# Mask tiles of a chunked recurrence: from 32 keys by 16 queries to 64 keys by 32 queries

## The chip, the cores and the metric

The kernel runs on one core of a Trainium2 chip. The metric is device time in microseconds (us) of one launch. TensorE is called PE here, VectorE DVE, ScalarE ACT, GpSimd POOL, SyncE SP. PEld is PE's weight load, which the profile lists beside the matmuls. The time before is 2788.95 us, the median of three runs (2788.55 to 2790.15).

## The reference

The reference is one step of a one-layer trunk: an RMS norm, a projection `x @ w_in` to nine groups of 1024 channels, a recurrence branch (HGRN2), a convolution branch (31 taps), two branch projections merged by gates, an output projection, and a gated embedding. It is computed for 2048 prompt tokens and for a sample group of 8 by 8 = 64 tokens. The change lies in the recurrence alone. For each of 8 heads, with 128 key channels:

```
S_t = diag(f_t) S_{t-1} + (1 - f_t) v_t^T          o_t = S_t^T q_t
attn[t, s] = sum_k q[t,k] (1 - f)[s,k] * prod_{s<u<=t} f[u,k]     for s <= t
o = attn @ v + (decayed q) @ S
```

`attn` is needed as blocks of 128 keys by 128 queries for prompt tokens, and as one 64 by 64 block for the sample group (eight independent sequences of 8 tokens).

## The kernel before, in words

**Stages.** The kernel runs, in order: the projection (`plan_head`, 8 heads in each of two token halves, up to about 1940 us), the two branch projections with the layer norm beside them (to about 2330 us), and the output stage. All large matmuls of the first two stages are issued at L1363, by a loop over units: a unit is one weight block against up to 512 tokens, 8 x 3 matmuls (the operands are split in a high and a low part). Behind each unit's 24 matmuls the loop issues whatever small jobs fall due in that unit. Due times are in units; `plan` of class `Hgrn` writes them by hand with `put(t, ...)`. Every engine works its own instructions in the order in which they are issued.

**The recurrence.** There are 32 `Hgrn` objects: 8 heads by 4 groups of 512 tokens. The last group of each head also carries the 64 sample tokens (`smp`), which makes 8 such objects and 24 without. The block of attention weights is built by doubling. Level h (1, 2, 4, ..., 64) joins each run of h keys with the h queries that follow it. DVE multiplies keys and queries of a level by their decays (`decay`, L436) and extends the running products (`grow`, L423). PE then forms the products over the 128 channels, and DVE copies the wanted entries out of PSUM under a mask (`evac_level`, L486).

**Tiles on PE before.** `mm_diag` (L448) takes 32 keys as weights against 32 queries. `mm_level` for h = 1 to 16 (L462) takes 32 keys as weights against the 16 queries of the same 32 tokens that are second halves. The four 32-token pieces of a chunk of 128 tokens write the output partitions 0, 32, 64 and 96 onward. For h = 32 two tiles of 32 by 32 a chunk, at output partitions 0 and 64, and for h = 64 one tile of 64 by 64 a chunk, at output partitions 0 to 63, are issued at L470. An output range of partitions is called a column strip in what follows: before, four strips of 32, and for h = 64 one strip of 64. Every f32 matmul of this kind has two records in the trace.

**Order.** `LVT` puts the matmuls of one object into three bursts: the diagonal with levels 1 and 2 (due at 2.0 units after the object's start), levels 4, 8 and 16 (4.25), levels 32 and 64 (5.4). The evacuations are due at 3.2 (diagonal, 1, 2), 4.9 (4, 8) and 5.85 (16). `gather` (ACT, L494 to L503) is due at 6.6 and copies the finished blocks into `at`, which `mm_o` at 9.0 uses as weights.

**Buffers.** PSUM tile `d32p` holds the diagonal and levels 1 to 8 of all chunks, `ab` holds level 16, 32 and 64. SBUF tile `d32` collects the 32 by 32 blocks (the trace names it `d`).

Of the kernel before, what the change touches and what calls it, by code (L numbers as in the profile page):

```python
# [17 lines left out]
P = 128  # L18
# [7 lines left out]
G = 512  # L26
# [6 lines left out]
LVT = ((2.0, (1, 2)), (4.25, (4, 8, 16)), (5.4, (32, 64)))  # L33
# [41 lines left out]
def view(t, off, dims):  # L75
    return bass.AP(t.tensor, t.offset + off, [list(t.ap[0])] + [list(d) for d in dims])
# [7 lines left out]
def tile_hybrid_step(  # L84
# [7 lines left out]
    nc = tc.nc  # L92
# [33 lines left out]
    ident = const.tile([P, P], F32, name="ident")  # L126
# [108 lines left out]
    oml = c1.tile([P, NH], F32, name="oml")  # L235
    lmx = c1.tile([P, NH], F32, name="lmx")
    cw = c1.tile([P, KB, 32], F32, name="cw")
    dmask = c1.tile([P, 32], F32, name="dmask")
    smask = c1.tile([NS, 8], F32, name="smask")
    lmask = {h: c1.tile([P, 16], I32, name=f"lmask{h}") for h in (1, 2, 4, 8, 16)}  # L240

    def bias(kind, j):
        c = UNIT_OF[kind] * 8 + j
# [26 lines left out]
    def set_masks():  # L270
        nc.vector.memset(onest, 1.0 / D)
        nc.vector.tensor_reduce(
            out=dmask, in_=ident.rearrange("p (a t) -> p t a", t=32), axis=mybir.AxisListType.X, op=ALU.add)
        for h, m in lmask.items():
            nb = 16 // h
            red = c1.tile([P, 16], F32, name="red", tag="red", bufs=2)
            nc.vector.tensor_reduce(
                out=red[:, 0:nb], in_=dmask.rearrange("p (b e i) -> p b e i", e=2, i=h)[:, :, 0, :],
                axis=mybir.AxisListType.X, op=ALU.add)
            nc.vector.tensor_copy(  # L280
                m.rearrange("p (b i) -> p b i", i=h), red[:, 0:nb].unsqueeze(2).broadcast_to([P, nb, h]))
        nc.vector.tensor_reduce(
            out=smask, in_=ident[0:NS, 0:NS].rearrange("p (b i) -> p b i", i=8), axis=mybir.AxisListType.X, op=ALU.add)
# [3 lines left out]
    at = c1.tile([P, 4, P], F32, name="at")  # L287
    at_s = c1.tile([NS, NS], F32, name="at_s")
    qm = c1.tile([P, 8, NS], F32, name="qm")
    s_all = c1.tile([P, NH, P], F32, name="s_all")  # L290
    tails = c1.tile([P, NH, 30], F32, name="tails")
    d32p = ps_1.tile([P, 5, 96], F32, name="d32p")
    nc.vector.memset(d32p, 0.0)

    for t in (lvl[0], lvl[1], lvl[2], at, at_s, qm, tails):
        nc.vector.memset(t, 0.0)
# [13 lines left out]
    blocks = []  # L310
# [44 lines left out]
    def lvl_row(h):  # L355
        i = (h.bit_length() - 1) % 6
        return lvl[i // 2][:, i % 2, :]

    class Hgrn:


        def __init__(self, j, tok0, smp):
            self.j, self.tok0, self.smp = j, tok0, smp
            self.n = 576 if smp else 512
            self.m = 5 if smp else 4
            self.kq = self.rp = self.v = self.za = None

        def alloc_kq(self):
# [66 lines left out]
                a, b = (view(t, 0, [[576 + h, 2], [2 * h, nb], [1, h]]) for t in (self.kq, self.rp))  # L435
            nc.vector.tensor_tensor(out=o, in0=a, in1=b, op=ALU.mult)  # L436

        def chunks(self, h):
            for c in range(4):
                yield c, 4  # L440
            if self.smp and h <= 4:
                yield 4, 2

        def mm_diag(self):
            for c, nq in self.chunks(0):
                for b in range(nq):
                    o = P * c + 32 * b
                    nc.tensor.matmul(  # L448
                        d32p[32 * b:32 * b + 32, c, 0:32], lhsT=self.kq[:, 0, o:o + 32], rhs=self.kq[:, 1, o:o + 32],
                        start=True, stop=True)  # L450

        def mm_level(self, h):
            lv = lvl_row(h)
            kk = self.kq[:, 0, :] if h == 1 else lv
            if h == 16:
                self.ab = ps_1.tile([P, 4, P], F32, tag="ab", name="ab")
            if h <= 16:
                dst, s = (self.ab, 0) if h == 16 else (d32p, 16 + 16 * h.bit_length())
                for c, nq in self.chunks(h):
                    for b in range(nq):  # L460
                        o = P * c + 32 * b
                        nc.tensor.matmul(  # L462
                            dst[32 * b:32 * b + 32, c, s:s + 16], lhsT=kk[:, o:o + 32],
                            rhs=lv[:, o:o + 32].rearrange("p (a e i) -> p a e i", e=2, i=h)[:, :, 1, :],
                            start=True, stop=True)
            else:
                for c in range(4):
                    for b in range(64 // h):
                        o = 2 * h * b
                        nc.tensor.matmul(  # L470
                            self.ab[o:o + h, c, o + h:o + 2 * h], lhsT=lv[:, P * c + o:P * c + o + h],
                            rhs=lv[:, P * c + o + h:P * c + o + 2 * h], start=True, stop=True)

        def evac_diag(self):
            m = self.m
            self.d32 = h1.tile([P, 5, 32], F32, tag="d32", name="d32")
            nc.vector.tensor_tensor(
                out=self.d32[:, 0:m], in0=d32p[:, 0:m, 0:32], in1=dmask.unsqueeze(1).broadcast_to([P, m, 32]),
                op=ALU.mult)

        def evac_level(self, h):
            m = 4 if h > 4 else self.m
            nb = 16 // h
            src = (view(self.ab, 0, [[P, 4], [16, 1], [1, 16]]) if h == 16 else
                   view(d32p, 16 + 16 * h.bit_length(), [[96, m], [h, nb], [1, h]]))
            nc.vector.copy_predicated(  # L486
                view(self.d32, h, [[32, m], [2 * h, nb], [1, h]]),
                view(lmask[h], 0, [[0, m], [h, nb], [1, h]]),
                src)

        def gather(self):
            for b in range(4):
                r = slice(32 * b, 32 * b + 32)
                nc.scalar.activation(out=at[r, :, r], in_=self.d32[r, 0:4, :], func=AF.Copy)  # L494
            for b in range(2):
                nc.scalar.activation(
                    out=at[64 * b:64 * b + 32, :, 64 * b + 32:64 * b + 64],
                    in_=self.ab[64 * b:64 * b + 32, :, 64 * b + 32:64 * b + 64], func=AF.Copy)
            nc.scalar.activation(out=at[0:64, :, 64:P], in_=self.ab[0:64, :, 64:P], func=AF.Copy)
            if self.smp:  # L500
                for b in range(2):
                    r = slice(32 * b, 32 * b + 32)
                    nc.scalar.activation(out=at_s[r, r], in_=self.d32[r, 4, :], func=AF.Copy)  # L503

        def final(self):
            n = self.n
# [114 lines left out]
        def plan(self, t0, tv):  # L621

            smp = self.smp
            ev = []

            def put(t, *fns):
                for fn in fns:
                    at_time(t0 + t, fn, 0)

            put(0.0, self.prep)  # L630
            for i, h in enumerate((1, 2, 4, 8, 16, 32, 64)):
                put(0.75 * i, lambda h=h: self.decay(h), lambda h=h: self.grow(h))
            for t, hs in LVT:
                put(t, *([self.mm_diag] if 1 in hs else []), *(lambda h=h: self.mm_level(h) for h in hs))
            put(3.2, self.evac_diag, lambda: self.evac_level(1), lambda: self.evac_level(2))
            put(4.9, lambda: self.evac_level(4), lambda: self.evac_level(8))
            put(5.25, self.final)
            put(5.85, lambda: self.evac_level(16))
            put(6.35, self.k_turn)
            put(6.6, self.gather)  # L640
            put(7.3, self.mm_kv)
            put(8.2, self.chain)
            put(9.0, self.mm_o)
            put(9.9, self.norm_o)
            put(11.2, self.turn_o)
            if smp:
                put(KTS, self.k_turn_sample)
                put(7.5, self.sample_o)
# [271 lines left out]
    for which, w, times, ev in (("a", w_br_a, t_a, evac_a), ("b", w_br_b, t_b, evac_b)):  # L920
        for hf in range(2):
# [151 lines left out]
    for i in range(9):  # L1073
        t, b = XOUT0 + XOUT_STEP * i, 8 + i
# [255 lines left out]
    for t, prio, n, fn in todo:  # L1330
        i = min(bisect.bisect_right(clock, t + 1e-6) - 1, len(units) - 1)
# [5 lines left out]
    for b in range(1, len(blocks)):  # L1337
        i = 1 if b == 2 else max(uses[b][0] - 3, 0)
# [133 lines left out]
```

## Time and profile before

| | us |
|---|---|
| median of 3 runs | 2788.95 |
| the profiled execution, its own time | 2788.37 |
| its span (first to last instruction) | 2786.6 |
| PE busy | 2754.3 |
| PE weight load busy | 2371.3 |
| DVE busy | 1943.8 |
| ACT busy | 931.4 |
| POOL busy | 283.4 |

1.8 us of the execution's time lie outside the span. The granted TensorE clock over the span is 0.998 of full speed. A busy share says how much of a stretch an engine had an instruction in flight. Matmuls overlap each other, so their mean durations are longer than the time that one adds; what one adds is read from the distance between starts.

### The profile page before, as it was taken

What the parts mean: (1) busy time and instruction counts of PE and PEld (TensorE: products, weight loads), DVE (VectorE), ACT (ScalarE), POOL (GpSimd) and SP (SyncE); (2) the same over time, 40 slices, a digit from 0 to 9 for tenths busy, and PEclk for the clock granted to TensorE, in tenths of its full rate; (3) what the DMA queues carried; (4) which work ended last, traced back from release to release, by engine and by line L of the source; (5) the groups of instructions that cost most, each with busy time, mean ns of one, the idle gap of its engine ahead of it and who ended that gap; (6) DMA issues with size and microseconds to landing.
All of it is one profiled execution on the core that took longest, in us unless ns stands there. A gap on an engine that the chain in (4) does not pass through costs nothing. (4 is left out here: it accounts for less than half of the span.)

```text
span 2786.6 us, 50684 instructions
## 1 busy us (share of the span) xinstructions
PE 2754.3 (99%) x21199; PEld 2371.3 (85%) x21199; DVE 1943.8 (70%) x3242; ACT 931.4 (33%) x2119; POOL 283.4 (10%) x441
## 2 busy tenths in 40 slices
PE   7999999999999999999999999999999999999998
PEld 6888888888888898989888998989889788788887
DVE  6577787877778787677778777688877775333433
ACT  5333333333333432223322323233254443322222
POOL 2001000000000000000000000000046410000000
PEclk9999999999999999999999999999999999999999
DMA  4222222222221422122222222123687788422321
GB/s 124 63 72 80 77 85 86 85 84 73 73 69 61 134 62 82 57 73 75 79 67 64 81 61 84 53 86 107 208 267 223 235 276 279 138 89 79 91 80 40
DMA packets 352797, 292.68 MB, mean 105 GB/s; under 512 B 17514, under 2 KB 301259, under 8 KB 352568
## 3 DMA queue, kind: packets, MB, share of 16 engines
q1 hardware_dynamic: 293856, 218.40, 26.0%
q10 hardware_dynamic: 58440, 70.86, 7.4%
q8 instruction: 166, 2.72, 0.4%
q14 instruction: 63, 0.52, 0.1%
q0 software_dynamic: 272, 0.19, 0.0%
HBM read 201.25 MB, written 88.14 MB: 104 GB/s over the span
## 5 line engine op out<-in xcount | busy, mean ns | idle before, releaser
L703 DVE SCALAR_TENSOR_TENSOR acc<-u,cw,acc 128x512 f32<-128x512 f32 x960 | 734.1, 765 | 20.7
L1363 PE MATMUL mm<-x1h,whi 128*128 128x320 f32 (+2 forms) x2112 | 708.2, 335 | 0.0
L1363 PE MATMUL mm<-x1h,wlo 128*128 128x320 f32 (+2 forms) x2112 | 691.1, 327 | 0.0
L1363 PE MATMUL mm<-x1l,whi 128*128 128x320 f32 (+2 forms) x2112 | 690.8, 327 | 0.0
L1363 PE MATMUL mm<-x0h,whi 128*128 128x512 f32 (+1 forms) x1416 | 563.3, 398 | 1.9 <-ACT x0h L1037 1.1
L1363 PE MATMUL mm<-x0l,whi 128*128 128x512 f32 (+1 forms) x1416 | 551.8, 390 | 1.8 <-DVE x0l L176 1.5
L1363 PE MATMUL mm<-x0h,wlo 128*128 128x512 f32 (+1 forms) x1416 | 551.7, 390 | 0.0
L1363 PEld LDWEIGHTS mm<-x1h,whi 128*128 128x128 f32 x2112 | 399.3, 189 | 33.8 <-ACT rp L376 4.5
L1363 PEld LDWEIGHTS mm<-x1h,wlo 128*128 128x128 f32 x2112 | 398.8, 189 | 28.2
L1363 PEld LDWEIGHTS mm<-x1l,whi 128*128 128x128 f32 x2112 | 399.4, 189 | 26.3
L327 DVE TENSOR_TENSOR wlo<-raw,whi 128x1024 fp32r<-128x1024 f32 x176 | 216.5, 1230 | 227.5 <-ACT whi L326 221.5
L1363 PEld LDWEIGHTS mm<-x0h,whi 128*128 128x128 f32 x1416 | 266.6, 188 | 59.3 <-ACT sp L786 2.6
L1363 PEld LDWEIGHTS mm<-x0h,wlo 128*128 128x128 f32 x1416 | 266.6, 188 | 57.0 <-DVE wlo L327 0.4
L1363 PEld LDWEIGHTS mm<-x0l,whi 128*128 128x128 f32 x1416 | 267.0, 189 | 53.3 <-DVE x0l L176 2.1
L326 ACT ACTIVATE whi<-raw 128x1024 fp32r<-128x1024 f32 x176 | 186.0, 1057 | 70.9 <-DVE mal L895 32.0
L1194 PE MATMUL ps<-woh,mgi 128*128 128x512 f32 x528 | 168.4, 393 | 2.0 <-DMA mgi<-mg_dr 2.0
L423 DVE TENSOR_TENSOR rp<-rp 128x512 f32<-128x512 f32 (+1 forms) x224 | 156.8, 700 | 9.6
L436 DVE TENSOR_TENSOR lvl<-kq,rp 128x512 f32<-128x512 f32 (+2 forms) x224 | 146.6, 655 | 1.9
L1194 PEld LDWEIGHTS ps<-woh,mgi 128*128 128x128 f32 x528 | 99.1, 188 | 22.9 <-DMA mgi<-mg_dr 2.2
L786 ACT ACTIVATE sp<-mm,vcol 128x512 f32<-128x512 f32 (+2 forms) x120 | 73.0, 608 | 130.8 <-PE mm L1363 117.2
L1268 DVE TENSOR_TENSOR g<-ps,g 128x512 f32<-128x512 f32 x32 | 22.1, 692 | 133.4 <-ACT g L1267 128.6
L567 POOL TENSOR_SCALAR ors<-oss 128x4 f32<-128x4 f32 (+1 forms) x40 | 10.7, 266 | 973.2 <-ACT on L565 973.2
(253 smaller groups left out, 3277.9 us busy)
## 6 DMA issues: line engine op xcount, KB each, us to landing
raw<-in_w_in_dram SPq DMA_DIRECT2D x144, 512.0 KB, 3.9
mgi<-mg_dr SPq DMA_DIRECT2D x16, 1024.0 KB, 6.1
gate<-am_dr SPq DMA_DIRECT2D x24, 512.0 KB, 5.7
mg_dr<-mg SPq DMA_DIRECT2D x24, 512.0 KB, 3.4
xt<-in_x_prompt_dram SPq DMA_DIRECT2D x16, 512.0 KB, 5.0
g_dr<-gst ACTq DMA_DIRECT2D x32, 256.0 KB, 2.8
cv_dr<-acc ACTq DMA_DIRECT2D x32, 256.0 KB, 2.1
raw<-in_w_br_a_dram SPq DMA_DIRECT2D x16, 512.0 KB, 5.4
```

Source lines behind the costliest of these rows:

```text
L326: nc.scalar.activation(out=b.hi, in_=b.raw, func=AF.Copy)
L327: nc.vector.tensor_tensor(out=b.lo, in0=b.raw, in1=f32(b.hi), op=ALU.subtract)
L423: nc.vector.tensor_tensor(out=io, in0=io, in1=tt, op=ALU.mult)
L436: nc.vector.tensor_tensor(out=o, in0=a, in1=b, op=ALU.mult)
L567: nc.gpsimd.tensor_scalar(out=rs[0:n, 0:m], in0=ss[0:n, 0:m], scalar1=1.0 / P, scalar2=EPS, op0=ALU.mult, op1=ALU.add)
L703: nc.vector.scalar_tensor_tensor(out=self.acc, in0=self.u[:, i:i + G], scalar=w, in1=self.acc, op0=ALU.mult, op1=ALU.add)
L786: nc.scalar.activation(out=s[:, 0:n], in_=ps[:, 0:n], func=func, bias=bias(kind, j))
L1194: nc.tensor.matmul(ps, lhsT=a[:, k, :], rhs=c[:, k, s], start=(k == 0 and i == 0), stop=(k == kn - 1 and i == len(ops) - 1))
L1268: nc.vector.tensor_tensor(out=g[0:n], in0=pp[0:n], in1=g[0:n], op=ALU.mult)
L1363: nc.tensor.matmul(ps[:, 0:u.n], lhsT=w[:, k, :], rhs=x[:, k, sl], start=(k == 0 and w is u.block.hi and x is xh), stop=(k == KB - 1 and w ...
```

## The change

Tiles of a level become 64 keys by 32 queries, tiles of the diagonal 64 by 64, and levels 1 to 32 go this way; h = 64 keeps its tile. A chunk of 128 tokens then has two pieces, at output partitions 0 and 64: two column strips of 64. The blocks are collected as 64 by 64 in `d`, so that `gather` copies two diagonal blocks and the h = 64 corner of a chunk instead of four blocks, two level-32 corners and the h = 64 corner. The masks `dmask` and `lmask` widen to 64 and 32 columns with one more level. The PSUM tiles become two full banks: `da` (diagonal, level 2, later 32 and 64) and `ab` (levels 1, 4, 8, 16, and the sample's diagonal, 1 and 2), and `ab` is taken at `mm_diag` instead of at level 16. The sample's level 4 is issued apart, with the third burst. The sample's evacuations are separate instructions. The set-up no longer clears `d32p`. The program is also built with `dynamic_dma_scratch_size=8192`. The due times of the bursts stay; level 32 joins level 16 in the evacuation at 5.85.

```
-        def chunks(self, h):
-            for c in range(4):
-                yield c, 4
-            if self.smp and h <= 4:
-                yield 4, 2
+        def blocks(self, h):
+            for c in range(4):
+                for b in range(2):
+                    yield P * c + 64 * b, 64 * b, c
+            if self.smp and h <= 4:
+                yield 512, 0, 4
+        def place(self, h, c):
+            if c == 4:
+                return ((da, 384) if h == 4 else (self.ab, {0: 384, 1: 448, 2: 480}[h]))
+            at, base = {0: (da, 0), 1: (da, 256), 2: (da, 384), 4: (self.ab, 0), 8: (self.ab, 128), 16: (self.ab, 256),
+                        32: (da, 0), 64: (da, 128)}[h]
+            return at, base + (32 if 0 < h < 64 else 64) * c
         def mm_diag(self):
...
+            for o, r, c in self.blocks(0):
+                bank, s = self.place(0, c)
+                nc.tensor.matmul(
+                    bank[r:r + 64, s:s + 64], lhsT=self.kq[:, 0, o:o + 64], rhs=self.kq[:, 1, o:o + 64],
+                    start=True, stop=True)
         def mm_level(self, h):
...
+            for o, r, c in self.blocks(h):
+                if c == 4 and h == 4:
+                    continue
+                bank, s = self.place(h, c)
+                if h < 64:
+                    nc.tensor.matmul(
+                        bank[r:r + 64, s:s + 32], lhsT=kk[:, o:o + 64],
+                        rhs=lv[:, o:o + 64].rearrange("p (a e i) -> p a e i", e=2, i=h)[:, :, 1, :],
+                        start=True, stop=True)
+                elif r == 0:
+                    nc.tensor.matmul(
+                        bank[0:64, s:s + 64], lhsT=lv[:, o:o + 64], rhs=lv[:, o + 64:o + P], start=True, stop=True)
...
+        def evac_level(self, h, c=0):
+            nb = 32 // h
+            n, m = (64, 1) if c == 4 else (P, 4)
+            bank, s = self.place(h, c)
             nc.vector.copy_predicated(
+                view(self.d[0:n], 64 * c + h, [[64, m], [2 * h, nb], [1, h]]),
+                view(lmask[h][0:n], 0, [[0, m], [h, nb], [1, h]]),
+                view(bank[0:n], s, [[32, m], [h, nb], [1, h]]))
...
+            put(LVT[2][0], self.mm_sample_4)
+            put(3.2, self.evac_diag, lambda: self.evac_levels((1, 2), (1, 2)))
+            put(4.9, lambda: self.evac_levels((4, 8), ()))
             put(5.25, self.final)
-            put(5.85, lambda: self.evac_level(16))
+            put(5.85, lambda: self.evac_levels((16, 32), (4,)))
```

## Rows read from the trace of the kernel before

**Rows 1.** The page: busy time of each engine with its share of the span and its instructions, and the granted TensorE clock in 40 equal slices of the span, in tenths.

```profile
PE 2754.3 (99%) x21199; PEld 2371.3 (85%) x21199; DVE 1943.8 (70%) x3242; ACT 931.4 (33%) x2119; POOL 283.4 (10%) x441
...
PEclk9999999999999999999999999999999999999999
```

**Rows 2.** Busy time of each engine in five stretches that cover the span: start, first and second half of the projection stage, branch projections, output stage. Columns: the stretch, its length, then busy us (and instructions) of PE, PEld, DVE, ACT and POOL, clock, DMA share, GB/s.

```profile
0.00:55.00 55.00, 41.00 (x218) 34.50 (x219) 38.93 (x70) 33.77 (x65) 15.55 (x40) 0.94 0.44 138
55.00:1000.00 945.00, 945.00 (x7978) 787.50 (x7977) 703.41 (x1067) 318.86 (x679) 50.17 (x76) 1.00 0.26 79
1000.00:1940.00 940.00, 940.00 (x8885) 845.50 (x8884) 720.52 (x1231) 288.30 (x678) 63.44 (x72) 1.00 0.24 72
1940.00:2330.00 390.00, 382.61 (x2040) 332.48 (x2040) 304.50 (x539) 163.25 (x346) 122.58 (x151) 1.00 0.78 247
2330.00:2786.60 456.60, 445.74 (x2087) 371.36 (x2085) 176.49 (x339) 127.25 (x352) 31.69 (x102) 1.00 0.33 102
```

**Rows 3.** Who waited for whom, PE's waits, the two longest: us in total, times, longest.

```profile
PE xtr L172 <- DVE xt L160: 11.7, 4, 9.2
PE rs L1016 <- POOL diag L1008: 5.3, 2, 4.9
```

**Rows 4.** Groups of instructions by line with shapes kept apart, PE, the matmuls of the mask over the whole span: weights as rows*columns, moving operand as partitions x columns, count of records | busy us, mean ns of one | idle before.

```profile
L462 PE MATMUL d32p<-lvl 128*32 128x16 f32 x3136 | 39.1, 185 | 0.0
...
L470 PE MATMUL ab<-lvl 128*64 128x64 f32 x256 | 21.7, 228 | 0.0
...
L462 PE MATMUL d32p<-lvl,kq 128*32 128x16 f32 x1056 | 15.4, 186 | 0.0
L448 PE MATMUL d32p<-kq 128*32 128x32 f32 x1056 | 15.2, 199 | 0.0
L462 PE MATMUL ab<-lvl 128*32 128x16 f32 x1024 | 14.9, 185 | 0.0
L470 PE MATMUL ab<-lvl 128*32 128x32 f32 x512 | 14.2, 199 | 0.0
```

**Rows 5.** Timeline of PE, the first burst of one object without sample tokens, between the last large matmul ahead of it and the first behind it. Columns here and in rows 6 to 9: start in us, us from the first start to the last end of the merged records, engine, line, operation, tiles, shapes, records.

```profile
93.59 0.39 PE L1363 MATMUL mm<-x0h,wlo 128*128 128x512 f32 x1
93.91 0.46 PE L448 MATMUL d32p<-kq 128*32 128x32 f32 x32
...
94.49 0.43 PE L462 MATMUL d32p<-lvl 128*32 128x16 f32 x30
94.86 0.50 PE L1363 MATMUL mm<-x0h,whi 128*128 128x512 f32 x1
```

**Rows 6.** The same view of the second burst of the same object.

```profile
107.26 0.39 PE L1363 MATMUL mm<-x1h,wlo 128*128 128x512 f32 x1
107.58 0.71 PE L462 MATMUL d32p<-lvl 128*32 128x16 f32 x62
...
108.51 0.50 PE L1363 MATMUL mm<-x1h,whi 128*128 128x512 f32 x1
```

**Rows 7.** The same view of a third burst, asked in narrow stretches so that single records stand apart: the 16 records of level 32, then the first, the second with the three after it, and the last of the 8 records of level 64, then the next large matmul.

```profile
806.83 0.45 PE L470 MATMUL ab<-lvl 128*32 128x32 f32 x16
...
807.20 0.27 PE L470 MATMUL ab<-lvl 128*64 128x64 f32 x1
807.31 0.40 PE L470 MATMUL ab<-lvl 128*64 128x64 f32 x4
...
807.66 0.22 PE L470 MATMUL ab<-lvl 128*64 128x64 f32 x1
807.81 0.50 PE L1363 MATMUL mm<-x1h,whi 128*128 128x512 f32 x1
```

**Rows 8.** The same view of an object with sample tokens: the first rows of its first and second burst, each with the large matmul behind the burst.

```profile
1006.10 0.53 PE L448 MATMUL d32p<-kq 128*32 128x32 f32 x36
...
1007.18 0.50 PE L1363 MATMUL mm<-x0h,whi 128*128 128x512 f32 x1
...
1020.10 0.77 PE L462 MATMUL d32p<-lvl 128*32 128x16 f32 x68
...
1021.08 0.39 PE L1363 MATMUL mm<-x1h,whi 128*128 128x256 f32 x1
```

**Rows 9.** Timeline of PE's weight loads in the layer norm's variance sum, whose matmuls have a single moving column: two neighbouring loads of 128 weight columns, then the two loads of 64 weight columns that follow.

```profile
2221.62 0.19 PEld L995 LDWEIGHTS vr<-onest,sum 128*128 128x128 f32 x1
2221.73 0.19 PEld L995 LDWEIGHTS vr<-onest,sum 128*128 128x128 f32 x1
...
2221.94 0.13 PEld L995 LDWEIGHTS vr<-onest,sum 128*64 128x64 f32 x1
2221.99 0.14 PEld L995 LDWEIGHTS vr<-onest,sum 128*64 128x64 f32 x1
```

**Rows 10.** The evacuations: two groups by line and shape on DVE (busy us, mean ns of one | idle before), the instructions of tile `d32p` that form the diagonal (min/median/max ns, first and last start), one group on ACT, and DVE's wait at the third burst.

```profile
L486 DVE COPY_PREDICATED d<-lmask,d32p 128x64 f32<-128x64 int32 x104 | 27.4, 263 | 30.4 <-PE d32p L462 27.6
...
L486 DVE COPY_PREDICATED d<-lmask,d32p 128x80 f32<-128x80 int32 x24 | 7.3, 303 | 0.6
...
L477 DVE TENSOR_TENSOR d<-d32p,dmask x32: 282/284/318, 57.0 to 1910.7; 128x128 f32<-128x128 f32 x24, 128x160 f32<-128x160 f32 x8
...
L494 ACT ACTIVATE at<-d 32x128 f32<-32x128 f32 x128 | 39.1, 305 | 8.1 <-DVE wlo L327 5.3 <-DVE d L486 1.6
...
DVE d L486 <- PE ab L470: 84.4, 15, 6.5
```

More of the change, by code (lines that the diff above doesn't have):

```diff
@@ L237, in tile_hybrid_step @@
     cw = c1.tile([P, KB, 32], F32, name="cw")
-    dmask = c1.tile([P, 32], F32, name="dmask")
+    dmask = c1.tile([P, 64], F32, name="dmask")
     smask = c1.tile([NS, 8], F32, name="smask")
-    lmask = {h: c1.tile([P, 16], I32, name=f"lmask{h}") for h in (1, 2, 4, 8, 16)}
+    lmask = {h: c1.tile([P, 32], I32, name=f"lmask{h}") for h in (1, 2, 4, 8, 16, 32)}
     def bias(kind, j):
@@ L272, in set_masks @@
         nc.vector.tensor_reduce(
-            out=dmask, in_=ident.rearrange("p (a t) -> p t a", t=32), axis=mybir.AxisListType.X, op=ALU.add)
+            out=dmask, in_=ident.rearrange("p (a t) -> p t a", t=64), axis=mybir.AxisListType.X, op=ALU.add)
         for h, m in lmask.items():
-            nb = 16 // h
-            red = c1.tile([P, 16], F32, name="red", tag="red", bufs=2)
+            nb = 32 // h
+            red = c1.tile([P, 32], F32, name="red", tag="red", bufs=2)
             nc.vector.tensor_reduce(
@@ L291, in tile_hybrid_step @@
     tails = c1.tile([P, NH, 30], F32, name="tails")
-    d32p = ps_1.tile([P, 5, 96], F32, name="d32p")
-    nc.vector.memset(d32p, 0.0)
+    da = ps_1.tile([P, G], F32, name="da")
     for t in (lvl[0], lvl[1], lvl[2], at, at_s, qm, tails):
@@ L364, in __init__ @@
             self.n = 576 if smp else 512
-            self.m = 5 if smp else 4
             self.kq = self.rp = self.v = self.za = None
@@ L436, in decay @@
             nc.vector.tensor_tensor(out=o, in0=a, in1=b, op=ALU.mult)
-        def chunks(self, h):
+        def blocks(self, h):
             for c in range(4):
-                yield c, 4
+                for b in range(2):
+                    yield P * c + 64 * b, 64 * b, c
             if self.smp and h <= 4:
-                yield 4, 2
-        def mm_diag(self):
[L445 to L450, printed above, removed]
+                yield 512, 0, 4
[5 more added lines that the diff above has]
+            return at, base + (32 if 0 < h < 64 else 64) * c
+        def mm_diag(self):
+            self.ab = ps_1.tile([P, G], F32, tag="ab", name="ab")
+            for o, r, c in self.blocks(0):
[3 more added lines that the diff above has]
+                    start=True, stop=True)
         def mm_level(self, h):
@@ L454, in mm_level @@
             kk = self.kq[:, 0, :] if h == 1 else lv
[L455 to L466, printed above, removed]
-                for c in range(4):
[L468 to L472, printed above, removed]
+            for o, r, c in self.blocks(h):
[10 more added lines that the diff above has]
+                        bank[0:64, s:s + 64], lhsT=lv[:, o:o + 64], rhs=lv[:, o + 64:o + P], start=True, stop=True)
@@ L474, in evac_diag, with mm_sample_4 @@
+        def mm_sample_4(self):
+            if self.smp:
+                bank, s = self.place(4, 4)
+                lv = lvl_row(4)[:, 512:576]
+                nc.tensor.matmul(
+                    bank[0:64, s:s + 32], lhsT=lv,
+                    rhs=lv.rearrange("p (a e i) -> p a e i", e=2, i=4)[:, :, 1, :], start=True, stop=True)
         def evac_diag(self):
-            m = self.m
-            self.d32 = h1.tile([P, 5, 32], F32, tag="d32", name="d32")
+            self.d = h1.tile([P, 5, 64], F32, tag="d", name="d")
@@ L477, in evac_diag @@
             nc.vector.tensor_tensor(
[L478 to L485, printed above, removed]
-            nc.vector.copy_predicated(
-                view(self.d32, h, [[32, m], [2 * h, nb], [1, h]]),
-                view(lmask[h], 0, [[0, m], [h, nb], [1, h]]),
-                src)
+                out=self.d[:, 0:4], in0=da[:, 0:256].rearrange("p (c t) -> p c t", c=4),
@@ new lines, in evac_diag @@
+                in1=dmask.unsqueeze(1).broadcast_to([P, 4, 64]), op=ALU.mult)
+            if self.smp:
+                nc.vector.tensor_tensor(
+                    out=self.d[0:64, 4], in0=self.ab[0:64, 384:448], in1=dmask[0:64], op=ALU.mult)
+        def evac_level(self, h, c=0):
+            nb = 32 // h
+            n, m = (64, 1) if c == 4 else (P, 4)
+            bank, s = self.place(h, c)
+            nc.vector.copy_predicated(
+                view(self.d[0:n], 64 * c + h, [[64, m], [2 * h, nb], [1, h]]),
+                view(lmask[h][0:n], 0, [[0, m], [h, nb], [1, h]]),
+                view(bank[0:n], s, [[32, m], [h, nb], [1, h]]))
@@ L491, in gather, with evac_levels @@
+        def evac_levels(self, hs, sample):
+            for h in hs:
+                self.evac_level(h)
+            for h in sample if self.smp else ():
+                self.evac_level(h, 4)
         def gather(self):
-            for b in range(4):
-                r = slice(32 * b, 32 * b + 32)
-                nc.scalar.activation(out=at[r, :, r], in_=self.d32[r, 0:4, :], func=AF.Copy)
             for b in range(2):
-                nc.scalar.activation(
-                    out=at[64 * b:64 * b + 32, :, 64 * b + 32:64 * b + 64],
-                    in_=self.ab[64 * b:64 * b + 32, :, 64 * b + 32:64 * b + 64], func=AF.Copy)
@@ L499, in gather @@
-            nc.scalar.activation(out=at[0:64, :, 64:P], in_=self.ab[0:64, :, 64:P], func=AF.Copy)
+                r = slice(64 * b, 64 * b + 64)
+                nc.scalar.activation(out=at[r, :, r], in_=self.d[r, 0:4, :], func=AF.Copy)
+            nc.scalar.activation(
+                out=at[0:64, :, 64:P], in_=da[0:64, 128:384].rearrange("p (c t) -> p c t", c=4), func=AF.Copy)
             if self.smp:
-                for b in range(2):
-                    r = slice(32 * b, 32 * b + 32)
-                    nc.scalar.activation(out=at_s[r, r], in_=self.d32[r, 4, :], func=AF.Copy)
+                nc.scalar.activation(out=at_s, in_=self.d[0:64, 4, :], func=AF.Copy)
@@ L634, in plan @@
                 put(t, *([self.mm_diag] if 1 in hs else []), *(lambda h=h: self.mm_level(h) for h in hs))
-            put(3.2, self.evac_diag, lambda: self.evac_level(1), lambda: self.evac_level(2))
-            put(4.9, lambda: self.evac_level(4), lambda: self.evac_level(8))
+            put(LVT[2][0], self.mm_sample_4)
+            put(3.2, self.evac_diag, lambda: self.evac_levels((1, 2), (1, 2)))
+            put(4.9, lambda: self.evac_levels((4, 8), ()))
             put(5.25, self.final)
-            put(5.85, lambda: self.evac_level(16))
+            put(5.85, lambda: self.evac_levels((16, 32), (4,)))
             put(6.35, self.k_turn)
@@ L1457 @@
     from concourse.bass_utils import run_bass_kernel_spmd as _run
-    nc = _bacc.Bacc("TRN2", target_bir_lowering=False, num_devices=1)
+    nc = _bacc.Bacc("TRN2", target_bir_lowering=False, num_devices=1, dynamic_dma_scratch_size=8192)
     arrays, args = {}, []
```

## The prediction

> **What bounds the kernel now.** I read the page's first part and then the stretches. PE is busy 2754.3 of 2786.6 us at the full granted clock, 2.4 GHz of its two levels [rows 1], and in the projection stage, where all of the change lies, it is busy 945.00 of 945.00 and 940.00 of 940.00 us, while DVE has 74 and 77% and ACT 34 and 31% [rows 2]. The list of waits says the same: PE's two longest stand at the start (L172) and in the layer norm (L1016) [rows 3]. So a nanosecond that PE's small matmuls add or free in this stage moves everything behind it by the same nanosecond. Whether PE's busy time shrinks is not to be read from the 185 to 228 ns means of the small matmuls, since they overlap: only distances between starts count. The groups give the number of records, 3136 + 1056 + 1056 + 1024 with 32 weight columns in four strips, 512 with 32 columns in two strips, 256 with 64 columns in one strip, 7040 in all [rows 4], two for each of 3520 matmuls.
>
> **What sets the price of one small record.** Take the bursts apart.
> - Four strips, 32 moving columns: 32 records in 0.46 us, the last of which lasts 0.20: (0.46 - 0.20)/31 = 8.4 ns each [rows 4, 5], 34 ns for each strip's turn.
> - Four strips, 16 moving columns: (0.71 - 0.18)/61 = 8.7 ns, 35 ns a strip [rows 4, 6]. Half the moving columns cost no less.
> - Two strips, 32 moving columns: (0.45 - 0.20)/15 = 16.7 ns, 33 ns a strip [rows 4, 7]. Half the strips take twice as long a record, so it isn't the number of records that the queue can pass.
> - One strip, 64 weight columns and 64 moving: from the second record at 807.31 to the eighth at 807.66 six steps, 58 ns each [rows 7].
> - One moving column: loads of 128 weight columns start 0.11 us apart, loads of 64 columns 0.05 us [rows 9].
>
> What is common to these is a price per strip that follows the weight columns: about 33 ns for 32, 55 to 58 for 64, 110 for 128, whatever moves against them up to that width. Strips work beside each other. The change halves the records but doubles the weight columns of each and halves the strips: each strip gets as many records as before, at 58 instead of 33 ns.
>
> The trace of before has no record with 64 weight columns and 32 moving ones, and no two strips of 64 at once. From below its price per strip is bounded by the two-strip row with the same moving width, 33 ns (and, if a record had a price of its own, by 17, twice 8.4); from above by 58 ns with each strip waiting for the other, 117 ns. I take 58 ns with both strips at once: the rows with equal weight columns say 55 to 58 for 64 moving columns and for a single one, and 32 lies between those.
>
> The Trainium skill states a rule that speaks against this change ("TensorE: Matmul & The Clock Gate", section on LDWEIGHTS): a weight load takes its number of columns divided by 1.2 in ns, and the contraction rows don't matter. That is 53 ns for 64 columns, an estimate from the page, where this trace has 58 between the records of [rows 7]; by it the sum below would be some 9 us smaller (5 ns on 58 steps of 32 objects).
>
> **The change, burst by burst** (first small start to the next large matmul; the 0.32 us from the large matmul ahead to the first small one stay [rows 5, 6]).
> - First burst: 16 diagonal records and twice 16 of levels 1 and 2, 24 for each strip. The first step of a 64-column burst is 0.11 us, the others 0.058, and from the last start to the large matmul it is 0.15 [rows 7]. That makes 0.11 + 22 x 0.058 + 0.03 (the other strip half a turn later) + 0.15 = 1.57 us, against 94.86 - 93.91 = 0.95 [rows 5]: +0.62.
> - Second burst, levels 4, 8, 16: again 24 for each strip, 1.57 against 108.51 - 107.58 = 0.93 [rows 6]: +0.64.
> - Third burst: 8 records of level 32 in each strip, and 8 of level 64, still in strip 0, so 16 there: 0.11 + 14 x 0.058 + 0.15 = 1.07 against 807.81 - 806.83 = 0.98 [rows 7]: +0.09. Little is lost here, since the step from 32 to 64 weight columns, which takes 0.2 us beyond the start of the last 32-column records (806.83 + 0.45 - 0.20 = 807.08 to the second 64-column record at 807.31), becomes an ordinary one.
> - Sum for one of the 24 objects without sample tokens: +1.35 us, together 32.4.
> - With sample tokens: the sample's diagonal and levels 1 and 2 add 6 records, all to strip 0: 1.57 + 6 x 0.058 = 1.92 against 1007.18 - 1006.10 = 1.08, +0.84. Second burst 1.57 against 1021.08 - 1020.10 = 0.98, +0.59 [rows 8]. The sample's level 4, moved to the third burst, adds two records there: 1.07 + 0.12 against 0.98, +0.21. Together +1.64, for 8 objects 13.1.
>
> Sum: 45.5 us.
>
> **What lies beside it.** DVE's masked copies grow from 64 to 128 columns. 64 to 80 columns cost 263 to 303 ns, 2.5 ns a column, so about 0.42 us, the diagonal's product at 256 columns likewise [rows 10]. An object goes from 0.28 + 5 x 0.26 = 1.6 to 7 x 0.42 = 2.9 us: +1.3, some 45 us over the stage with the sample's separate copies. They lie under PE: DVE has about 460 us free there [rows 2], and stands waiting for the third burst for 84.4 us, so it runs ahead of PE [rows 10]. The users come late: the evacuation of level 32 is due at 5.85, the gather at 6.6 and the matmul that needs it at 9.0, more than two units of 24 large matmuls later. If that cover were gone PE would stand for the 1.3 us of each object, 40 us more; I cost it at 0, as no wait of PE for DVE is listed in this stage [rows 3]. ACT's gather loses two of its four 0.3 us copies of blocks and both corner copies [rows 10]; ACT is idle two thirds of the stage, so nothing comes of it. The two PSUM tiles are rewritten by the next object's first burst, more than a unit after the last reader: 0. The set-up (one clear less, one more mask, the DMA scratch size) lies in the first 55 us, where PE waits for the norm; -1 to +2 us, taken as 0.
>
> The profiled execution took 2788.37 us, 0.6 below the median. 2788.4 + 45.5 = 2833.9; from the median 2834.5. I predict 2834.
>
> **Rivals.**
> - A record has its own price (5%), the one case on the other side. If the records pass at 8.4 ns whatever their weights, 6784 of them (all but level 64) become 3648: 3136 x 8.4 = 26 us less, and 3 us for the step between tile widths in 32 third bursts: 2760. For it: 8.4 and 8.7 ns in both four-strip rows. Against it: 16.7 ns in the two-strip row. It decides where a strip's turn of 64 weight columns stays under some 31 ns.
> - The moving columns set the price (5%): 58 ns for the diagonal, 33 for the levels. Then an object gains 8 x 25 = 0.2 us in the diagonal and gives back 0.1 to 0.2 in the third burst, the sample adds about 1 us over all: some 3 us, 2792. Against it: the 16-column records cost no less than the 32-column ones, and loads with one moving column keep their distance. The Trainium skill speaks for this one ("TensorEngine Tiling (Array Packing)", section Instruction Overhead): a matmul has an overhead of about 60 cycles and one moving column takes as long as 60. By that rule the weights don't enter. Of the rows only those with 32 weight columns agree with it; the distances in [rows 9] don't.
> - The two strips of 64 don't work beside each other (4%): then the second strip's 56 records of an object come on top, 56 x 0.058 x 32 = 104 us, 2938. Against it: four strips of 32 do overlap [rows 5], and so do two [rows 7].
>
> **How the numbers follow.** The forecast has 86%. Its own uncertainty: 55 instead of 58 ns takes 6 us off; 5% on the turn, as between 33 and 35 ns above, adds 5; bursts begin and end within 0.05 us of what I used, 5 us over 96 bursts. That gives 2822 to 2844, and since the rivals hold 14% together I leave them out. A measurement tells about 0.2% (5.6 us) from no change: slower by more has 0.90 (forecast and third rival), within it 0.05 (second rival), faster 0.05 (first).
>
> **What would show it.** The first and second burst of an object take 1.55 to 1.6 us; pairs of records with 64 weight columns start 58 ns apart, one in each strip; the count of mask records falls to 3904; PE stays fully busy through a projection stage that is 45 us longer; DVE's share there hardly moves. It is wrong if level records with 32 moving columns come at 33 ns a strip, if two strips alternate, or if PE shows waits for the masked copies.

## The result, and the profile after

The changed kernel takes 2831.11 us, the median of four runs (2830.23 to 2833.52), where the kernel before takes 2789.14 (2788.55 to 2790.15): the ratio is 1.0148, with a 95% interval of 1.0135 to 1.0161. It is 42 us slower; 45 us were forecast, and 2834 us as the time.

On the page of the changed kernel PE has 3136 matmul records less, 18063 for 21199 [rows 1], and is busy for 45 us more, 2799.8 for 2754.3. (The profiled execution is the slowest of the four, 2833.52 us, with a span of 2831.7, 45.1 above the span before.)

```profile
PE 2799.8 (99%) x18063; PEld 2416.8 (85%) x18063; DVE 1974.1 (70%) x3307; ACT 902.0 (32%) x1983; POOL 283.5 (10%) x441
```

In the two halves of the projection stage (columns as in rows 2) PE is busy in every microsecond; the stage now runs to about 1984 us. DVE's share there is 74 and 77%, as before.

```profile
55.00:1000.00 945.00, 945.00 (x6206) 790.39 (x6204) 699.57 (x1056) 297.52 (x599) 45.47 (x75) 1.00 0.25 78
1000.00:1984.00 984.00, 984.00 (x7540) 887.49 (x7539) 756.62 (x1308) 279.23 (x623) 68.25 (x73) 1.00 0.24 71
```

The timeline of PE shows where the time is. The lines that answer to rows 5, 6, 7 and 8, in this order: the first burst of one object, its second and its third, and the three of an object with sample tokens (columns as there). L456 is the diagonal here, L468 the levels up to 32, L473 level 64, and L1376 a large matmul.

```profile
95.15 0.69 PE L456 MATMUL da<-kq 128*64 128x64 f32 x16
95.66 0.61 PE L468 MATMUL da<-lvl,kq 128*64 128x32 f32 x16
96.10 0.64 PE L468 MATMUL da<-lvl 128*64 128x32 f32 x16
96.67 0.50 PE L1376 MATMUL mm<-x0h,whi 128*128 128x512 f32 x1
...
109.36 1.59 PE L468 MATMUL ab<-lvl 128*64 128x32 f32 x48
110.88 0.50 PE L1376 MATMUL mm<-x1h,whi 128*128 128x512 f32 x1
...
116.99 0.66 PE L468 MATMUL da<-lvl 128*64 128x32 f32 x16
117.47 0.66 PE L473 MATMUL da<-lvl 128*64 128x64 f32 x8
118.06 0.50 PE L1376 MATMUL mm<-x0h,whi 128*128 128x512 f32 x1
...
1026.98 0.69 PE L456 MATMUL da<-kq 128*64 128x64 f32 x16
...
1028.85 0.50 PE L1376 MATMUL mm<-x0h,whi 128*128 128x512 f32 x1
...
1041.80 1.59 PE L468 MATMUL ab<-lvl 128*64 128x32 f32 x48
1043.32 0.39 PE L1376 MATMUL mm<-x1h,whi 128*128 128x256 f32 x1
...
1049.71 0.66 PE L468 MATMUL da<-lvl 128*64 128x32 f32 x16
...
1050.87 0.41 PE L1376 MATMUL mm<-x1h,whi 128*128 128x320 f32 x1
```

Read the distance from the first small record to the next large matmul, not the busy time. The second burst has 48 records with 64 weight columns where there were 96 with 32, and lasts 110.88 - 109.36 = 1.52 us for 0.93 [rows 6]. One such record lasts 0.22 us, so (1.59 - 0.22)/47 = 29 ns lie between two starts. With two strips that is 58 ns for a strip's turn, the distance between two records of the same strip, with 32 moving columns. Per object without sample tokens: 1.52 - 0.95 = 0.57, 1.52 - 0.93 = 0.59, 1.07 - 0.98 = 0.09, together 1.25 us; with sample tokens 1.87 - 1.08 = 0.79, 1.52 - 0.98 = 0.54, and 1.16 - 0.98 = 0.18 for the third burst (in the kernel before it takes 0.98 us with sample tokens or without), together 1.51. Then 24 x 1.25 + 8 x 1.51 = 42.1 us. All 96 bursts of the two traces, added up, give 93.1 us before and 135.3 after, 42.2 more. The medians differ by 42.0.

The two profiled executions differ by 45.1. At the last matmul of the projection (tile `os`, 1942.6 us before, 1984.3 after) it is 41.7. The rest comes mostly at the start of the output stage, where PE waits 2.7 us for `mgi` (2.0 before) and the mean granted clock is 0.98 over the 100 us from 2400 on (1.00 over the matching 104 us from 2356 on before). The change doesn't touch that stage.

The copies grew less than they were costed: 0.29 to 0.42 us each where 0.42 was taken for all, and DVE is busy for 30 us more, 1974.1 for 1943.8, where 45 were forecast. PE still has no wait for them in this stage. Three groups of DVE on the evacuations, by line and shape, with the idle time before them, and PE's three longest waits, all three outside the projection stage:

```profile
L497 DVE COPY_PREDICATED d<-lmask,da 128x128 f32<-128x128 int32 x96 | 38.2, 397 | 82.2 <-PE da L473 78.5
L497 DVE COPY_PREDICATED d<-lmask,ab 128x128 f32<-128x128 int32 x96 | 28.2, 294 | 41.7 <-PE ab L468 40.4
L486 DVE TENSOR_TENSOR d<-da,dmask 128x256 f32<-128x256 f32 x32 | 13.4, 418 | 3.7 <-PE da L468 3.7
```

```profile
PE xtr L172 <- DVE xt L160: 11.1, 4, 9.2
PE rs L1029 <- POOL diag L1021: 5.3, 2, 4.9
PE ps L1207 <- DMA mgi<-mg_dr: 2.7, 1, 2.7
```

It is DVE that waits, 78.5 us, for PE's third burst, as before [rows 10].

### The profile page after: what moved, and what is told of

It reads as the page before. It is cut to its first block, busy times and chain, and to the rows that moved or that the text cites. A ratio compares the mean times of both kernels' runs of the same rounds, so it can differ in the third digit from the quotient of the medians.

```text
span 2831.7 us, 44360 instructions
## 1 busy us (share of the span) xinstructions
PE 2799.8 (99%) x18063; PEld 2416.8 (85%) x18063; DVE 1974.1 (70%) x3307; ACT 902.0 (32%) x1983; POOL 283.5 (10%) x441
## 5 line engine op out<-in xcount | busy, mean ns | idle before, releaser
L1376 PE MATMUL mm<-x1h,whi 128*128 128x320 f32 (+2 forms) x2112 | 708.2, 335 | 0.0
L1376 PE MATMUL mm<-x1h,wlo 128*128 128x320 f32 (+2 forms) x2112 | 691.3, 327 | 0.0
L1376 PE MATMUL mm<-x1l,whi 128*128 128x320 f32 (+2 forms) x2112 | 690.6, 327 | 0.0
L1376 PE MATMUL mm<-x0h,whi 128*128 128x512 f32 (+1 forms) x1416 | 563.9, 398 | 1.5 <-ACT x0h L1050 1.1
L1376 PE MATMUL mm<-x0l,whi 128*128 128x512 f32 (+1 forms) x1416 | 552.3, 390 | 1.7 <-DVE x0l L176 1.3
L1376 PE MATMUL mm<-x0h,wlo 128*128 128x512 f32 (+1 forms) x1416 | 552.5, 390 | 0.0
L1376 PEld LDWEIGHTS mm<-x1h,whi 128*128 128x128 f32 x2112 | 399.3, 189 | 33.9 <-ACT rp L374 3.8
L1376 PEld LDWEIGHTS mm<-x1h,wlo 128*128 128x128 f32 x2112 | 398.9, 189 | 28.3
L1376 PEld LDWEIGHTS mm<-x1l,whi 128*128 128x128 f32 x2112 | 399.6, 189 | 26.4
L1376 PEld LDWEIGHTS mm<-x0h,whi 128*128 128x128 f32 x1416 | 267.3, 189 | 59.0 <-ACT sp L799 2.6
L1376 PEld LDWEIGHTS mm<-x0h,wlo 128*128 128x128 f32 x1416 | 267.1, 189 | 56.9 <-DVE wlo L326 0.4
L1376 PEld LDWEIGHTS mm<-x0l,whi 128*128 128x128 f32 x1416 | 267.6, 189 | 53.6 <-DVE x0l L176 2.2
```

The lines of the kernel that those rows point to most:

```text
L1376: nc.tensor.matmul(ps[:, 0:u.n], lhsT=w[:, k, :], rhs=x[:, k, sl], start=(k == 0 and w is u.block.hi and x is xh), stop=(k == KB - 1 and w ...
```

## The experiments

Every time below is a median, and every ratio is to the kernel before in the same runs, 2790.5 to 2790.7 us there.

**Weights of 32 keys in the changed kernel.** This takes back the one thing that the theory blames and leaves everything else of the change in place.

```
-                        bank[r:r + 64, s:s + 32], lhsT=kk[:, o:o + 64],
-                        rhs=lv[:, o:o + 64].rearrange("p (a e i) -> p a e i", e=2, i=h)[:, :, 1, :],
-                        start=True, stop=True)
+                    for e in (0, 32):
+                        nc.tensor.matmul(
+                            bank[r + e:r + e + 32, s:s + 32], lhsT=kk[:, o + e:o + e + 32],
+                            rhs=lv[:, o:o + 64].rearrange("p (a e i) -> p a e i", e=2, i=h)[:, :, 1, :],
+                            start=True, stop=True)
```

(The diagonal and the sample's level 4 likewise.)

> The changed kernel with each tile of 64 keys issued as two of 32 keys (weights), against the same 32 queries (64 for the diagonal), so that each output strip of 64 partitions becomes two of 32; results, buffers, masks, evacuations and the gather are those of the changed kernel. Theory (a strip's turn takes the larger of weight and moving columns: 33 ns for 32, 58 ns for 64, and strips work beside each other): levels fall back to 33 ns a strip with four strips; the diagonal keeps 58 ns, since 64 columns move. First burst about 1.15 us, second 0.93, third 0.98: 2795 us (2789 plus 32 x 0.2), records of the mask up from 3904 to 7552. Rival, a record has its own price of 29 ns as in the changed kernel: twice the records, some 100 us slower than the changed kernel, 2930. Rival, the wider masked copies on DVE cost PE time: the time stays at 2815 or above although the bursts shrink.

Measured 2797.64 us, ratio 1.0029 (1.0018 to 1.0040). Its first and second burst on PE's timeline:

```profile
94.63 0.65 PE L457 MATMUL da<-kq 128*32 128x64 f32 x32
95.10 0.45 PE L470 MATMUL da<-lvl,kq 128*32 128x32 f32 x30
...
95.78 0.50 PE L1379 MATMUL mm<-x0h,whi 128*128 128x512 f32 x1
...
108.51 1.03 PE L470 MATMUL ab<-lvl 128*32 128x32 f32 x96
109.47 0.51 PE L1379 MATMUL mm<-x1h,whi 128*128 128x512 f32 x1
```

The second burst is back at 0.96 us (0.93 before the change) with 96 records for 48, so twice the records are no cost by themselves, and half of them no gain. The first takes 1.15 us: the diagonal's records have 32 weight columns and 64 moving, and (0.65 - 0.22)/31 = 14 ns in four strips make a turn of 55 to 58 ns. In these runs the turn follows the larger of the two widths. DVE's wide copies are all still there (DVE is busy for 1973.7 us), and they cost PE nothing: what remains above the kernel before, 7 to 8 us, is no more than its bursts have grown by, 9 us over its trace, mostly the diagonal's 0.2 us in 32 objects. The time is 3 us above the 2795 expected.

**Half the moving columns.**

```
-                        bank[r:r + 64, s:s + 32], lhsT=kk[:, o:o + 64],
-                        rhs=lv[:, o:o + 64].rearrange("p (a e i) -> p a e i", e=2, i=h)[:, :, 1, :],
-                        start=True, stop=True)
+                        bank[r:r + 64, s:s + 16], lhsT=kk[:, o:o + 64], rhs=lv[:, o + 32:o + 48],
+                        start=True, stop=True)
```

> The changed kernel with only 16 of the 32 queries moving in every tile of levels 1 to 32 (and the sample's), and masked copies of half the columns: half of the off-diagonal products are left out, so the output is not the reference's. Weights stay 64 keys. Theory: no change of the turn, 58 ns, so 2831 us (2828 to 2832; the first step of a burst may be 0.01 to 0.02 us shorter). Rival, the moving columns set the price: half of them gives up to 48 x 13 ns a strip and object back, some 20 us, 2811. Rival, DVE's wider copies cost time: half of them gone gives part of the 42 us back, 2815.

Measured 2830.99 us, ratio 1.0145 (1.0132 to 1.0159), the time of the changed kernel. Of its first burst, to be held against the first one above:

```profile
95.66 0.60 PE L468 MATMUL da<-lvl,kq 128*64 128x16 f32 x16
96.10 0.62 PE L468 MATMUL da<-lvl 128*64 128x16 f32 x16
96.65 0.50 PE L1375 MATMUL mm<-x0h,whi 128*128 128x512 f32 x1
```

The starts are the same to 0.02 us. With 64 weight columns it makes no difference whether 32 or 16 move, and masked copies of half the width gave nothing back either.

**Diagonal of 64 keys, levels of 32.** Only the `for e in (0, 32)` around the level's matmuls (and the sample's level 4) of the first experiment is kept.

> The changed kernel with the levels' tiles issued as two of 32 keys and the diagonal left at 64 keys by 64 queries, two strips of 64. Against the variant that splits the diagonal too, only the strip width changes inside the first burst. Theory: the diagonal's turn is 58 ns either way, and the step from strips of 64 to strips of 32 costs about 0.1 us as in the third burst of the kernel before: 32 x 0.1 to 0.15 above that variant, 2798 to 2801 us. Rival, narrower diagonal strips are dearer by the record: this one is faster than that variant, 2785 to 2792.

Measured 2806.47 us, ratio 1.0058 (1.0044 to 1.0071), above the range given. The first burst has a gap where the strips change:

```profile
95.11 0.69 PE L456 MATMUL da<-kq 128*64 128x64 f32 x16
95.72 0.46 PE L469 MATMUL da<-lvl,kq 128*32 128x32 f32 x32
96.00 0.49 PE L469 MATMUL da<-lvl 128*32 128x32 f32 x32
96.42 0.50 PE L1378 MATMUL mm<-x0h,whi 128*128 128x512 f32 x1
```

It takes 1.31 us, 0.16 more than with four strips throughout, which makes 5 us over 32 objects, where 3 to 5 had been allowed. Some 0.1 of the 0.16 stand at the step itself: the last diagonal start is at 95.11 + 0.69 - 0.22 = 95.58 and the first level start 0.14 later, against 0.04 in the first experiment (94.63 + 0.65 - 0.22 = 95.06 to 95.10). The direction is that of the theory. The medians of the two variants are 8.8 us apart, the spans of the profiled executions 8.4. Of these 5.5 are there at the last matmul of the projection (`os`, 1951.5 and 1957.0 us). The rest comes behind it: at the start of the output stage PE waits 3.5 us for `mgi` in place of 2.0, and from 2400 to 2440 us the mean granted clock is 0.96 in place of 1.00. Whether it is so in the other executions, and why, stays open.

**Levels 32 and 64 over four strips, in the kernel before.** If a strip's turns set the time, the kernel before wastes some itself: its level 32 uses two strips of four and its level 64 one of two.

```
+            elif h == 32:
+                for c in (0, 2, 1, 3):
+                    for b in range(2):
+                        o, r = P * c + 64 * b, 64 * b + 32 * (c // 2)
+                        nc.tensor.matmul(
+                            self.ab[r:r + 32, c, 32:64], lhsT=lv[:, o:o + 32], rhs=lv[:, o + 32:o + 64],
+                            start=True, stop=True)
             else:
-                for c in range(4):
-                    for b in range(64 // h):
...
+                for c in (0, 2, 1, 3):
+                    for b in range(2):
+                        o, r = P * c + 32 * b, 64 * (c // 2) + 32 * b
+                        nc.tensor.matmul(
+                            self.ab[r:r + 32, c, 64:P], lhsT=lv[:, o:o + 32], rhs=lv[:, P * c + 64:P * c + P],
+                            start=True, stop=True)
...
+            for g in range(2):
+                c = slice(2 * g, 2 * g + 2)
+                for b in range(2):
+                    r = 64 * b + 32 * g
+                    nc.scalar.activation(
+                        out=at[64 * b:64 * b + 32, c, 64 * b + 32:64 * b + 64], in_=self.ab[r:r + 32, c, 32:64],
+                        func=AF.Copy)
+                nc.scalar.activation(out=at[0:64, c, 64:P], in_=self.ab[64 * g:64 * g + 64, c, 64:P], func=AF.Copy)
```

> The kernel before, with levels 32 and 64 spread over all four strips of 32: level 64 as two tiles of 32 keys by 64 queries a chunk, chunks 0 and 1 at output partitions 0 and 32, chunks 2 and 3 at 64 and 96; level 32 of chunks 2 and 3 at output partitions 32 and 96; the gather moves the blocks back with six copies on ACT instead of three. Theory: a strip has 4 turns of 33 ns and 4 of 58 ns in the third burst in place of 8 of 33, a width step of 0.1 us and 8 of 58: 0.53 to 0.58 us for 0.98, 32 x 0.40 to 0.45 = 13 to 14.5 us faster than before, 2775. Rival, the turn is set by the number of records: 16 + 16 records at 8.4 ns each way, and the gain is only the width step and the single strip's wait, 3 to 8 us. Rival, ACT's three more copies (about 0.8 us an object) delay the matmul behind the gather: no gain, 2789 or above.

Measured 2776.88 us, ratio 0.9951 (0.9939 to 0.9964): faster than both kernels. Its third burst, which answers to rows 7:

```profile
114.97 0.33 PE L470 MATMUL ab<-lvl 128*32 128x32 f32 x16
115.12 0.41 PE L477 MATMUL ab<-lvl 128*32 128x64 f32 x16
115.46 0.50 PE L1373 MATMUL mm<-x0h,whi 128*128 128x512 f32 x1
```

It takes 0.49 us for 0.98 with eight records more, below the 0.53 to 0.58 expected. 32 x 0.49 = 16 us; 13.6 were measured, where the price by the record allowed 3 to 8. PE has no wait for ACT's added copies in this stage.

**Two bursts, and one, in place of three.** Both start from the four-strip kernel.

```
-LVT = ((2.0, (1, 2)), (4.25, (4, 8, 16)), (5.4, (32, 64)))
+LVT = ((2.0, (1, 2)), (5.4, (4, 8, 16, 32, 64)))
...
-            put(4.9, lambda: self.evac_level(4), lambda: self.evac_level(8))
...
-            put(5.85, lambda: self.evac_level(16))
+            put(5.85, *(lambda h=h: self.evac_level(h) for h in (4, 8, 16)))
```

> The kernel of the four-strip run (levels 32 and 64 over four strips of 32) with the second and third burst merged into one at 5.4 units, and the evacuations of levels 4 and 8 moved to 5.85. Theory: a burst costs, beside its records, the step from a large matmul to the first small one (0.32 for 0.23 us), the wait from the last small start to the next large matmul (0.11 for a turn of 0.03), and a longer first step of the large ones (0.34 for 0.23): some 0.28 us, 32 of them 9 us: 2768 us. Rival: DVE, whose copies of levels 4 and 8 now come later and in one row with level 16, delays the gather, and PE waits for it at the matmul due at 9.0: no gain, 2777 or above, with PE waits in the projection stage.

Measured 2769.84 us, ratio 0.9925 (0.9913 to 0.9938), the fastest version of the study that computes all. 7 us were gained of the 9 expected, from bursts saved and not from records.

```
+LVT = ((5.4, (1, 2, 4, 8, 16, 32, 64)),)
...
+    lvl = [c1.tile([P, 2 if i < 3 else 1, 576], F32, name=f"lvl{i}") for i in range(4)]
...
+        i = h.bit_length() - 1
...
+            put(5.45, self.final)
+            put(5.85, self.evac_diag, *(lambda h=h: self.evac_level(h) for h in (1, 2, 4, 8, 16)))
```

(The evacuations due at 3.2 and 4.9 move to 5.85 there, and the DMA scratch is 8192 to make room for the seventh row.)

> As the merged run, with all levels and the diagonal in one burst at 5.4 units, a seventh row for the level operands, the in-place product of keys and queries at 5.45 and all evacuations at 5.85. Theory: two bursts less an object, 18 us below the four-strip run: 2759 us. Rival: the in-place product on DVE now waits for the burst, and PE's transposes of its result (due at 6.35) wait for DVE: up to 1.2 us an object, 2777 to 2800, with PE waits at the transposes of the keys.

Measured 2837.28 us, ratio 1.0158 (1.0144 to 1.0172). Neither theory nor rival: the time lies above the rival's 2777 to 2800 too, and there is no wait at the transposes of the keys (L527). Two of PE's longest waits, and its busy time by stretches:

```profile
PE ab L462 <- issue: 15.8, 7, 2.7
PE d32p L462 <- issue: 12.3, 7, 2.2
```

```profile
55.00:1000.00 945.00, 919.02 (x7794) 770.39 (x7793) 692.17 (x1039) 321.42 (x712) 49.03 (x75) 0.99 0.25 78
1000.00:1940.00 940.00, 914.39 (x8847) 825.76 (x8847) 692.17 (x1198) 289.07 (x698) 59.97 (x71) 0.99 0.23 69
```

PE stands still for 52 us of these 1885, in the middle of the bursts and even of a level, and "issue" means that the profile shows nothing that it waited for. One such place on PE's timeline, and the DMA queues in the stretch from 114 to 119 us (packets, MB, share of the 16 engines):

```profile
116.20 0.18 PE L462 MATMUL ab<-lvl 128*32 128x16 f32 x1
118.40 0.22 PE L462 MATMUL ab<-lvl 128*32 128x16 f32 x4 [2.02 <-issue]
```

```profile
q8 instruction: 1, 0.02, 1.4%
```

The only packet of that stretch is one of 16 KB on the instruction queue. That suggested that a long row of short instructions outruns their supply. The whole trace bears this out better than one place does. 21 of the 32 bursts stop inside (the expectation below has nearly every one), for 1.8 to 2.7 us each; one of these stops is put down to DVE, the others to "issue". In each of the 21 a packet of that queue starts between 0.7 us before the stop and 0.5 us after its start, and ends before PE goes on; a packet takes 1.0 us (median). The queue carries one packet for every 255 to 256 of PE's records, matmuls and weight loads together, in all nine kernels (166 for 42398 before, 141 for 36126 in the changed kernel). A burst of 224 matmuls has 448 such records and passes in 2.2 us where it isn't stopped: 1.75 packets' worth. A burst of 128 has 256.

**A shorter burst.** The last run tests the supply against a wait for DVE. It starts from the one-burst kernel.

```
-                put(t, *([self.mm_diag] if 1 in hs else []), *(lambda h=h: self.mm_level(h) for h in hs))
+                put(t, *([self.mm_diag] if 1 in hs else []), *(lambda h=h: self.mm_level(h) for h in hs if h not in (2, 4, 8)))
```

> The one-burst kernel with the matmuls of levels 2, 4 and 8 left out on PE (their part of the mask stays zero, so the output is not the reference's); the burst falls from 216 to 120 records (232 to 124 with sample tokens), while every instruction on DVE and ACT, its order and what it waits for stay. In the one-burst run PE stands for some 2 us inside nearly every burst, mid-level, with no wait shown, while a 16 KB packet of the instruction queue is under way. Theory: the burst uses up instructions faster than they arrive; 120 records don't. Then the standing time is gone, bursts take 1.3 to 1.4 us, the granted clock stays full in the projection stage, and the time is the 2759 us expected of one burst less 32 x 0.8 us of records: 2733 us. Rival: PE stands for DVE, whose work is unchanged: the stops stay, some 2810 us.

Measured 2737.94 us, ratio 0.9809 (0.9792 to 0.9825). (The burst has 224 records with all levels and 128 without the three, 8 more each than the expectation says.) PE in the same two stretches of the stage:

```profile
55.00:1000.00 945.00, 940.23 (x6782) 790.45 (x6781) 734.62 (x1104) 335.40 (x751) 56.35 (x78) 1.00 0.26 81
1000.00:1875.00 875.00, 875.00 (x7156) 791.54 (x7155) 675.39 (x1173) 284.50 (x689) 58.29 (x70) 1.00 0.24 73
```

PE's waits in these two stretches, all of them:

```profile
PE o L568 <- DVE st L553: 2.2, 1, 2.2
PE ab L477 <- DVE lvl L436: 1.2, 1, 1.2
PE mm L1371 <- DVE x0l L205: 1.2, 1, 1.2
```

The stops without a named reason are gone with DVE's work unchanged, so they weren't waits for DVE; the 5 us that PE still stands are three waits for it by name. The time is 5 us above the 2733 expected and 72 below the rival's. So it is the longer burst that makes PE stop, and not one of its levels: 4 and 8 pass without such stops in the merged run's bursts of 128, but for one of 0.3 us. That it is the supply of instructions fits the packets at all 21 stops, but was not tried by itself.

## Why the prediction was right

- **The bound.** PE's added distance came through: 42.1 us from the bursts, 41.7 at the end of the projection in the profiled pair, 42.0 between the medians. That the last agrees to a tenth is luck, as the 3 us behind the projection show. That the stage is PE's alone was read rightly from rows 2 and 3.
- **The price of a strip's turn.** 58 ns for 64 weight columns with 32 moving: forecast 58, measured 58 (29 ns a record in two strips). This was the open cost, bounded from 33 to 117 ns, and choosing the rows with equal weight columns over the row with equal moving width was right. The runs with 32 keys (2797.64) and with 16 moving columns (2830.99) show it from both sides. The sentence "whatever moves against them up to that width" holds with its limit: with 64 moving columns the 32-key diagonal takes a turn of 55 to 58 ns.
- **The term that was too large.** Each 64-column burst was put at 1.57 us and takes 1.52, a little under the 1.55 to 1.6 that were to show it. The second strip starts 0.01 rather than 0.03 us after the first. The other 0.03 differ by burst: the second burst's first step is 0.08 us where 0.11 was taken from a burst with 64 moving columns, and in the first burst, whose diagonal does begin with 0.11, the first turn of the levels behind it takes 0.03 us and not 0.058. Over the bursts that makes 45.5 for 42.1 us, well inside the range of 2822 to 2844.
- **The third burst** takes 1.07 us as worked out, since the width step between level 32 and 64 is gone. That such a step has a price of its own is shown, the other way round, by the run with a 64-key diagonal: 0.16 us a burst, some 0.1 of it at the step.
- **The cover.** DVE's wider copies cost PE nothing, seen in the changed kernel by PE's waits and in the run with 32 keys by the time. Their own cost was put too high, 45 us for 30: 128 columns were priced at 420 ns from copies out of `d32p` [rows 10], and now the copies out of `da` take 397 and those out of `ab` 294. As the term was costed at 0, nothing came of it.
- **The rivals.** A price by the record falls with the 32-key run, which has nearly twice the records of the changed kernel and is 33 us faster. A price by the moving columns falls with the changed kernel itself; the rule in the Trainium skill ("TensorEngine Tiling (Array Packing)", section Instruction Overhead) that one moving column takes as long as 60, cited for it, has no step between 33 and 58 ns in it either, and it doesn't describe these bursts, where with 32 moving columns each time 32 weight columns took 33 ns and 64 took 58. Two strips of 64 do work beside each other: 29 ns a record is half of one strip's 58.

## What to carry to other kernels

Price a small matmul by distances between starts, strip by strip, and look for the width that these follow before counting instructions: here halving their number raised each one's turn from 33 to 58 ns and halved the strips. Tiles that leave strips empty are the ones to spread; levels 32 and 64 gave 14 us that way, and merging bursts another 7. Don't merge too far: a burst of 224 records stopped PE where 128 did not.

## What the runs showed of the hardware that was not expected

Inside one long burst of small matmuls PE stops for about 2 us with no wait that the profile names: 2.02 us before 118.40 in the one-burst run, some 52 us over the projection stage up to 1940 us, with a 16 KB packet on the instruction queue at each of the 21 stops inside a burst. In the two runs with bursts of 128 to 136 records there is one stop without a named wait, of 0.3 us. A lower clock goes with the stops: its mean over the profiled execution is 0.987 of full speed there, against 0.997 to 0.998 in the changed kernel and the kernel before. The run missed 2759 us by 78; 52 of them are standing time, and that the lower clock is the rest is an estimate (1.1% of 2836 us is 31). A change of strip width inside a burst costs some 0.1 us at the step from 64 to 32, and the burst that has it is 0.16 us longer.
